# Chunk inputs laid out by neighbouring groups in DRAM, loaded for two groups in one run, with a third buffer for them and for the S5 tables

## The chip, the cores and the metric

One core of one Trainium2 chip runs the whole program in one launch. The metric is the device time in microseconds (us) of one execution. Engines are named as in the profile: PE (TensorE matmul), PEld (its weight load), DVE (VectorE), ACT (ScalarE), POOL (GpSimd), SP (SyncE, which here only issues DMAs). A DMA that SP or ACT issues is carried by up to 16 DMA engines; they are called lanes here.

## The reference: what is computed

One layer of a hybrid block on 2048 tokens of width 1024, with 256 context tokens as a prefix. The part around the change is the S5 branch:

```
z = (rmsnorm(h) * (1 + sc) + sh) @ w_in          # split into u_s5, g_s5, u_lru, g_lru
u: 1024 channels = 64 groups of 16               # S5 groups, state 64, two directions
h_t = abar * h_(t-1) + bbar u_t                  # complex scan, forward and backward, from the context's state
y = Re(C h) + d * u ;  y = gelu(y) ;  y = y * sigmoid(y @ w_glu + b_glu)
out = h + gt * ([y_s5 * silu(g_s5), y_lru * silu(g_lru)] @ w_out), then a final rmsnorm
```

All inputs and the output are float32.

## The kernel before

The S5 scan is done in chunks of T = 16 tokens: 2304 tokens are NCH = 144 chunks. Per group of 16 channels the kernel needs the chunk inputs u (128 partitions = 16 channels by 8 positions, for two halves `kt` of a chunk, 144 chunks), a table `wt` that takes a chunk's inputs to its state, a table `et` that takes states to outputs, and a table `mt` that takes a chunk's inputs to its outputs directly.

The program runs in these stages, with times of the profiled execution:

- `projections(0, ...)`, to about 600 us: matmuls of the input projection for the context and the first half of the tokens (lines 248 to 250 in `mm3`, tile `pp`), eight blocks of 128 channels for each of four kinds. Woven into it are the tables of the S5 branch, which go to DRAM: `ED`, `KD`, and `WD` (line 661, stored by POOL for two groups at a time). A block of kind `u_s5` copies its results into `zsc` (context, 16 chunks) and `zst` (64 chunks), and SP stores them to the DRAM tensor `ZU` (lines 330 and 348, two DMAs each, one for each `kt`). `zst` has one buffer: the next block's first copy into it waits until both stores have landed. The eight blocks of `u_s5` lie at about 247 to 385 us.
- `projections(1, ...)`, to about 1113 us, for the second half of the tokens, with the RG-LRU branch (`lru`) beside it. Its eight `u_s5` blocks lie at about 837 to 955 us.
- `s5_inputs` for groups 0 to 31 (`sin[0]`) and 32 to 63 (`sin[1]`), about 982 to 1146 us, woven into the last projections. For each group: four products with `wt` and u into `pw` (line 743), then four ACT copies into the scan's tile z (lines 746 to 750).
- `s5_scan`, 144 steps of three DVE instructions (lines 771, 773, 775), one scan for each half of the groups. The first needs all of `sin[0]`.
- `s5_outputs` for each half of the groups, about 1226 to 1441 us: ACT copies the states into `h` (lines 800, 801), PE makes `py` from u with `mt` (line 806) and from `h` with `et` (line 808). `out_lru` (tile `po`) is woven into the scans and the outputs as side work of PE.
- `glu` and `tail`, the last 370 us.

Each engine executes its instructions in program order, SP among them: a DMA whose buffer is not yet free keeps back all later DMAs of SP. The order of the instructions on an engine follows the generators that `merge` interleaves, with priorities from the scheduling layer. `load_u` (line 754) loads the inputs of four groups by two DMAs into one of two buffers; `wt` and `et` (tag `t2`, lines 736 and 788) are loaded for two groups at a time into one of two buffers. So the table of groups 4 and 5 can start to load when PE is done with groups 0 and 1.

The layout in DRAM: `ZU` is [2, 1024 channels, 8, 144], so one partition's inputs of four groups are four runs of 576 bytes. `WD` is [64, 128, 512], two runs of 2 KB for two groups.

Of the kernel before, what the change touches and what calls it, by code (L numbers as in the profile page):

```python
# [9 lines left out]
F32 = mybir.dt.float32  # L10
# [6 lines left out]
P = 128  # L17
D = 1024
# [5 lines left out]
G = 64  # L24
NCH = 144
T = 16
# [20 lines left out]
class Block:  # L47
# [204 lines left out]
    def projections(self, half, kinds):  # L252

        nc = self.nc
        win = self.io["w_in"].rearrange("o (k p) n -> p (o k) n", p=P)
        base = {"u_s5": 0, "g_s5": D, "u_lru": 2 * D, "g_lru": 3 * D}

        kept = {"u_lru": 0, "g_lru": 8, "u_s5": 16}

        def load(i):  # L260

            if i >= len(blocks):
                return None
            kind, b = blocks[i][:2]
            if half and kind in kept:
                w = self.wp.tile([P, 2, KT, P], F32R, tag="w", bufs=2, name="w")
                nc.sync.dma_start(out=w.rearrange("p s k n -> p (s k n)").bitcast(F32), in_=self.WS[kept[kind] + b])
                return w
            cs = base[kind] + b * P
            return self.wload(win[:, :, cs:cs + P])  # L270

        def split(raw, i):
            kind, b, tiles = blocks[i]
            if half and kind in kept:
                return raw
            with self.tc.high_priority(offset=250):
                w = self.wsplit(raw, nc.scalar.copy)
            if not half and kind in kept and tiles[-1] == both[-1]:
                nc.gpsimd.dma_start(out=self.WS[kept[kind] + b], in_=w.rearrange("p s k n -> p (s k n)").bitcast(F32))
            return w  # L280

        both = [2 * half, 2 * half + 1]
        blocks = []
        for group in kinds:
            if group == ("g_s5",) and half:
                blocks += [("g_s5", b, [t]) for t in both for b in range(8)]
            else:
                blocks += [(kind, b, ["c"] + both if half == 0 and kind[0] == "u" else both)
                           for b in range(8) for kind in group]
        if half == 0:  # L290
            blocks.remove(("g_lru", 0, both))
            blocks[:1] = [("u_lru", 0, ["c", 0]), ("g_lru", 0, [0]), ("u_lru", 0, [1]), ("g_lru", 0, [1])]
        raw, nxt = self.first if half == 0 else (load(0), None)
        w = split(raw, 0)
        raw = nxt or load(1)
        for i, (kind, b, tiles) in enumerate(blocks):
            whi, wlo = w[:, 0], w[:, 1]
            r = slice(b * P, (b + 1) * P)
            if kind == "u_lru" and tiles[0] != 1:
                u = self.conv_input(half, b)  # L300
            if kind == "u_s5":
                st = self.stp.tile([P, T, 64], F32, tag="st4", bufs=1, name="zst")
            for tl in tiles:
                n = 256 if tl == "c" else 512
                xh, xl = self.xh[tl]
                ps = self.psM.tile([P, 512], F32, tag="mm", name="pp")
                for k in range(KT):
                    self.mm3(ps[:, :n], lambda k: whi[:, k, :], lambda k: wlo[:, k, :],
                             lambda k: xh[:, k, :n], lambda k: xl[:, k, :n], (k,))
                    if k < KT - 1:  # L310
                        yield
                if kind == "u_lru":
                    pos = 1 if tl == "c" else (3 if half else LC + 4) + tl % 2 * 512
                    nc.scalar.copy(out=u[:, pos:pos + n], in_=ps[:, :n])  # L314
                    if tl == "c":
                        self.conv(half, b, u, 0)
                elif kind == "g_lru":
                    o = self.stp.tile([P, 512], F32, tag="st2", bufs=2, name="ust")
                    if half:
                        nc.scalar.activation(out=o, in_=ps, func=AF.Sigmoid)  # L320
                        nc.vector.tensor_mul(out=o, in0=ps, in1=o)
                    else:
                        nc.scalar.activation(out=o, in_=ps, func=AF.Silu)
                    nc.scalar.dma_start(out=self.GL[r, tl * 512:tl * 512 + 512], in_=o)
                elif kind == "u_s5":
                    if tl == "c":
                        sc = self.stp.tile([P, T, 16], F32, tag="st2", bufs=2, name="zsc")
                        nc.scalar.copy(out=sc[:, ::-1, :], in_=ps[:, :256].rearrange("p (c j) -> p j c", j=T))
                        for kt in range(2):
                            nc.sync.dma_start(out=self.ZU[kt, r, :, 0:16], in_=sc[:, kt * 8:kt * 8 + 8, :])  # L330
                    else:
                        o = (tl % 2) * 32
                        nc.scalar.copy(out=st[:, ::-1, o:o + 32], in_=ps.rearrange("p (j r) -> p j r", j=T))
                else:
                    o = self.stp.tile([P, 512], F32, tag="st2", bufs=2, name="gst")
                    nc.scalar.activation(out=o.rearrange("p (j a r) -> p a j r", j=8, a=2),
                                         in_=ps.rearrange("p (a j r) -> p a j r", a=2, j=8), func=AF.Silu)
                    nc.scalar.dma_start(out=self.GS[tl, r].rearrange("d j c -> d (j c)"), in_=o)
                if tl == tiles[0] and i + 1 < len(blocks):
                    w = split(raw, i + 1)  # L340
                    raw = load(i + 2)
                yield
            if kind == "u_lru" and tiles[-1] == both[-1]:
                self.conv(half, b, u)
            if kind == "u_s5":
                cs = slice(80, NCH) if half else slice(16, 80)
                for kt in range(2):
                    nc.sync.dma_start(out=self.ZU[kt, r, :, cs], in_=st[:, kt * 8:kt * 8 + 8, :])


    def conv_input(self, half, b):
# [266 lines left out]
    def s5_tables(self, tp):  # L618

        nc, v = self.nc, self.nc.vector  # L620
# [29 lines left out]
        def transposed(gp, W):  # L650
            Wt = tp.tile([P, 2, 2, 2, P], F32, tag="Wt", bufs=2, name="Wt")
            for g in range(2):
                ps = self.psT.tile([P, 512], F32, tag="t", name="psw")
                for kt in range(2):
                    for c in range(2):
# [2 lines left out]
                                            W[:, kt, g, c].rearrange("p h j -> p (h j)"),  # L658
                                            self.ident)
                nc.scalar.copy(out=Wt[:, g].rearrange("p k c m -> p (k c m)"), in_=ps)  # L660
            nc.gpsimd.dma_start(out=self.WD[2 * gp:2 * gp + 2].rearrange("g p a -> p g a"),
                                in_=Wt.rearrange("p g k c m -> p g (k c m)"))

        def lags(gq, E):

# [60 lines left out]
    def s5_inputs(self, gp, zt, hb):  # L726

        nc = self.nc
        for gl in range(32):
            g = hb * 32 + gl  # L730
            gi = gl % 2
            if gl % 4 == 0:
                u4 = self.load_u(gp, g)
            u = u4[:, :, gl % 4]
            if gi == 0:
                w = gp.tile([P, 2, 2, 2, P], F32, tag="t2", bufs=2, name="wt")
                nc.sync.dma_start(out=w.rearrange("p g k c m -> p g (k c m)"),
                                  in_=self.WD[g:g + 2].rearrange("g p a -> p g a"))
            ps = self.psM.tile([P, 512], F32, tag="mm", name="pw")
            pw = ps[:, :2 * NCH].rearrange("p (c n) -> p c n", c=2)  # L740
            for c in range(2):
# [11 lines left out]

    def load_u(self, gp, g):

        u = gp.tile([P, 2, 4, NCH], F32, tag="u", bufs=2, name="u")
        for kt in range(2):
            src = self.ZU[kt, g * 16:(g + 4) * 16].rearrange("(g h) j c -> (h j) g c", g=4)
            self.nc.sync.dma_start(out=u[:, kt], in_=src)
        return u  # L760

    def s5_scan(self, sp, zt, hb):
# [15 lines left out]
    def s5_outputs(self, gp, go, zt, hb):  # L778

        nc = self.nc  # L780
        for gl in range(32):
            g = hb * 32 + gl
            gi = gl % 2
            if gl % 4 == 0:
                u4 = self.load_u(gp, g)
            u = u4[:, :, gl % 4]
            if gi == 0:
                e = gp.tile([P, 2, 2, T, T], F32, tag="t2", bufs=2, name="et")
                src = self.ED[g // 4].rearrange("p (c a) -> p c a", c=2)[:, :, g % 4 * 256:g % 4 * 256 + 512]
                nc.sync.dma_start(out=e.rearrange("p c g j h -> p c (g j h)"), in_=src)  # L790
                ps = self.psM.tile([P, 512], F32, tag="mm", name="py")
                py = ps.rearrange("p (g a n) -> p g a n", g=2, a=2)
# [249 lines left out]
    def build(self):  # L1042
        tc, nc = self.tc, self.nc
        with ExitStack() as es:
# [4 lines left out]
            self.XC = dt("XC", [D, LC + L])  # L1049
            self.GL = dt("GL", [D, L])  # L1050
            self.YL = dt("YL", [D, L])
            self.ZU = dt("ZU", [2, D, 8, NCH])
            self.GS = dt("GS", [4, D, T, 32])
            self.YT = dt("YT", [G, T, 8, 2, P])
            self.ZD = dt("ZD", [D, 8, 2, P])
# [1 line left out]
            self.HP = dt("HP", [T, P, D])  # L1057
            self.WS = dt("WS", [24, P, 2 * KT * P])
            self.ED = dt("ED", [G // 4, P, 2048])
            self.WD = dt("WD", [G, P, 512])  # L1060
            self.KD = dt("KD", [G, T, 31, T])
            self.psM = pool(es, "psM", bufs=4, space=PSUM)
            self.psG = pool(es, "psG", bufs=2, space=PSUM)
# [152 lines left out]
```

## Time and profile before

| what | value |
|---|---|
| runs | 1814.55, 1817.27, 1821.26 us (median 1817.27) |
| profiled execution | 1820.46 us, span 1818.7 us |
| PE busy | 1703.3 us, 94% of the span |
| DVE, ACT busy | 1112.1 us (61%), 873.6 us (48%) |
| granted clock of TensorE, mean | 0.977 |
| DMA | 373.55 MB, mean 205 GB/s |

The span is the time from the first to the last instruction; 1.8 us of the profiled execution lie around it. The busy share of PE is high nearly everywhere, so time is saved mainly where PE stands still or where its clock is lower. The share of the DMA engines is the mean over the 16 lanes.

### The profile page before, as it was taken

How to read it: one execution, taken by the hardware profiler on the slowest of the kernel's cores; microseconds unless marked ns; L12 is line 12 of the kernel's file. 1: busy time of each engine (PE TensorE's matmuls, PEld its weight loads, DVE VectorE, ACT ScalarE, POOL GpSimd, SP SyncE). 2: the span in 40 equal slices, each digit the busy share in tenths (PEclk: the TensorE clock that was granted, in tenths of full speed). 3: DMA queues.
4: the chain of work that ended last, by engine and by line, in shares of the span. 5: the costliest groups of instructions: out<-in, count | busy, mean ns of one | idle time of the engine just before them, and what ended most of it. 6: DMA issues, size and time to landing. Idle time of an engine off the chain costs nothing.

```text
span 1818.7 us, 25980 instructions
## 1 busy us (share of the span) xinstructions
PE 1703.3 (94%) x9785; PEld 1365.7 (75%) x9785; DVE 1112.1 (61%) x2006; ACT 873.6 (48%) x1382; POOL 138.3 (8%) x268
## 2 busy tenths in 40 slices
PE   7787989999999899999998997989999999999997
PEld 2565777888888565656666786779988899998886
DVE  4789989985023268887667058898501166336663
ACT  2623332222365288787775888416555443222221
POOL 1022212211100000000000000000000000001121
PEclk9898999999999899999999998999999999999999
DMA  8685558877646545666777788528888757456562
GB/s 255 153 215 199 206 197 258 261 250 261 186 132 211 155 150 211 200 217 210 219 200 221 241 249 257 163 82 256 268 270 250 226 179 215 142 159 217 188 198 88
DMA packets 335470, 373.55 MB, mean 205 GB/s; under 512 B 124029, under 2 KB 274161, under 8 KB 323058
## 3 DMA queue, kind: packets, MB, share of 16 engines
q1 hardware_dynamic: 288304, 243.43, 46.9%
q0 software_dynamic: 20672, 94.91, 13.7%
q10 hardware_dynamic: 26370, 33.57, 5.3%
q8 instruction: 77, 1.26, 0.3%
q14 instruction: 47, 0.39, 0.1%
HBM read 233.49 MB, written 138.35 MB: 204 GB/s over the span
## 4 chain that ended last, share of the span: by engine, by line
PE 54%; issue 17%; DMA 11%; DVE 10%; ACT 5%; SPq 1%; POOL 1%; ACTq 0%; DVEq 0%; POOLq 0%
PE pp L248 7%; PE pp L249 7%; PE pp L250 7%; PE po L250 4%; PE po L248 4%; PE po L249 4%; PE pgl L249 3%; PE pgl L250 3%; PE pgl L248 3%; PE py L808 2%; DMA et<-ED 2%; PE py L806 2%; PE pw L743 2%; DMA wt<-WD 2%; DVE p L771 2%
## 5 line engine op out<-in xcount | busy, mean ns | idle before, releaser
L248 PE MATMUL pp<-x,w 128*128 128x512 f32 x1024 | 422.1, 413 | 13.4 <-ACT uc L314 13.0
L250 PE MATMUL pp<-x,w 128*128 128x512 f32 x1024 | 406.8, 397 | 2.6 <-DVE w L241 2.6
L249 PE MATMUL pp<-x,w 128*128 128x512 f32 x1024 | 406.8, 397 | 0.0
L248 PEld LDWEIGHTS pp<-x,w 128*128 128x128 f32 x1024 | 194.8, 190 | 114.7 <-issue 63.6
L250 PEld LDWEIGHTS pp<-x,w 128*128 128x128 f32 x1024 | 194.5, 190 | 45.3 <-DVE w L241 3.5
L249 PEld LDWEIGHTS pp<-x,w 128*128 128x128 f32 x1024 | 195.2, 191 | 37.2 <-DVE x L213 1.0
L241 DVE TENSOR_TENSOR w<-wraw,w 128x1024 fp32r<-128x1024 f32 x66 | 80.5, 1220 | 158.9 <-ACT w L240 151.4
L240 ACT CAST w<-wraw 128x1024 fp32r<-128x1024 f32 x66 | 69.1, 1047 | 142.8 <-PE pp L250 97.5
L248 PE MATMUL po<-x,w 128*128 128x512 f32 x256 | 103.3, 403 | 0.8 <-ACT z L750 0.6
L743 PE MATMUL pw<-u,wt 128*128 128x144 f32 x512 | 79.0, 304 | 23.7 <-DMA wt<-WD 16.2
L250 PE MATMUL po<-x,w 128*128 128x512 f32 x256 | 100.2, 391 | 1.0 <-DVE w L241 1.0
L249 PE MATMUL po<-x,w 128*128 128x512 f32 x256 | 99.9, 390 | 0.4 <-DVE x L839 0.4
L248 PE MATMUL po<-ws,yh 128*128 128x512 f32 x256 | 99.6, 389 | 0.0
L249 PE MATMUL po<-ws,yh 128*128 128x512 f32 x256 | 99.6, 389 | 0.0
L250 PE MATMUL po<-ws,yl 128*128 128x512 f32 x256 | 99.6, 389 | 0.0
L743 PEld LDWEIGHTS pw<-u,wt 128*128 128x128 f32 x512 | 74.4, 203 | 31.8 <-ACT z L750 12.6
L422 PE MATMUL pg<-xc,gw 64*64 64x512 f32 (+1 forms) x320 | 89.8, 581 | 8.9 <-DMA GL<-ust 8.4
L422 PE MATMUL pg<-xs,gw 64*64 64x512 f32 (+1 forms) x320 | 88.5, 581 | 4.0 <-ACT gi L426 4.0
L808 PE MATMUL py<-h,et 128*128 128x128 f32 x512 | 80.0, 280 | 12.9 <-ACT h L801 9.4
L379 DVE SCALAR_TENSOR_TENSOR xcv<-uc,vcol,xcv 128x256 f32<-128x256 f32 (+2 forms) x72 | 72.9, 1012 | 22.6 <-ACT xcv L376 21.9
L771 DVE TENSOR_TENSOR p<-z,A 128x128 f32<-128x128 f32 x288 | 77.8, 287 | 5.3
L808 PEld LDWEIGHTS py<-h,et 128*128 128x128 f32 x512 | 68.7, 195 | 14.9 <-ACT h L801 12.2
(258 smaller groups left out, 3520.5 us busy)
## 6 DMA issues: line engine op xcount, KB each, us to landing
wraw<-in_w_in_dram SPq DMA_DIRECT2D x50, 512.0 KB
WS<-w POOLq DMA_DIRECT2D x24, 1024.0 KB, 7.0
w<-WS SPq DMA_DIRECT2D x24, 1024.0 KB
u<-ZU SPq DMA_DIRECT2D x64, 288.0 KB
ED<-E POOLq DMA_DIRECT2D x16, 1024.0 KB, 5.5
WD<-Wt POOLq DMA_DIRECT2D x32, 512.0 KB, 4.3
wt<-WD SPq DMA_DIRECT2D x32, 512.0 KB
et<-ED SPq DMA_DIRECT2D x32, 512.0 KB
```

The costliest lines, as they stand in the source:

```text
L240: copy(out=w[:, 0], in_=raw)
L241: self.nc.vector.tensor_sub(out=w[:, 1], in0=raw, in1=w[:, 0])
L248: nc.tensor.matmul(ps, lhsT=whi(k), rhs=xhi(k), start=(k == 0), stop=False)
L249: nc.tensor.matmul(ps, lhsT=whi(k), rhs=xlo(k), start=False, stop=False)
L250: nc.tensor.matmul(ps, lhsT=wlo(k), rhs=xhi(k), start=False, stop=(k == KT - 1))
L379: nc.vector.scalar_tensor_tensor(out=xc, in0=u[:, o + k:o + k + N], scalar=cw[:, k * 8 + b:k * 8 + b + 1], in1=xc, op0=ALU.mult, op1=ALU.add)
L422: nc.tensor.matmul(pss[w][e * 64:e * 64 + 64, :n], lhsT=gw[ws, d, e, :], rhs=xcs[(w + e) % 2][ws, o:o + n], start=True, stop=True, tile_po ...
L743: nc.tensor.matmul(pw[:, c, :], lhsT=w[:, gi, kt, c, :], rhs=u[:, kt, :], start=(kt == 0), stop=(kt == 1))
L771: v.tensor_mul(out=p, in0=cur.unsqueeze(1).to_broadcast([P, 2, 2, 32]), in1=self.A16[:, :, :, gs])
L806: nc.tensor.matmul(o, lhsT=ms(m[:, i * 8:i * 8 + T]), rhs=u[:, i, 16:], start=(i == 0), stop=False)
L808: nc.tensor.matmul(o, lhsT=ms(e[:, i, gi]), rhs=h[:, i, :], start=False, stop=(i == 1))
```

## The change

`ZU` becomes [2, 16, 8, 64, 144]: for each channel of a group and each position in a chunk half, the 64 groups stand side by side. The stores of `zsc` and `zst` write the same bytes in the same runs of 64 and 256 bytes, addressed by group first. `load_u` loads two groups instead of four, by two DMAs with one run of 1152 bytes per partition, into one of three buffers. `WD` becomes [32, 128, 1024], one run of 4 KB per partition. `wt` and `et` get a third buffer.

```diff
-                            nc.sync.dma_start(out=self.ZU[kt, r, :, 0:16], in_=sc[:, kt * 8:kt * 8 + 8, :])
+                            nc.sync.dma_start(out=self.ZU[kt, :, :, b * 8:b * 8 + 8, 0:16].rearrange("h j g c -> g (h j) c"),
+                                          in_=sc[:, kt * 8:kt * 8 + 8, :])
...
-                    nc.sync.dma_start(out=self.ZU[kt, r, :, cs], in_=st[:, kt * 8:kt * 8 + 8, :])
+                    nc.sync.dma_start(out=self.ZU[kt, :, :, b * 8:b * 8 + 8, cs].rearrange("h j g c -> g (h j) c"),
+                                      in_=st[:, kt * 8:kt * 8 + 8, :])
...
-            nc.gpsimd.dma_start(out=self.WD[2 * gp:2 * gp + 2].rearrange("g p a -> p g a"),
-                                in_=Wt.rearrange("p g k c m -> p g (k c m)"))
+            nc.gpsimd.dma_start(out=self.WD[gp], in_=Wt.rearrange("p g k c m -> p (g k c m)"))
...
-            if gl % 4 == 0:
-                u4 = self.load_u(gp, g)
-            u = u4[:, :, gl % 4]
             if gi == 0:
-                w = gp.tile([P, 2, 2, 2, P], F32, tag="t2", bufs=2, name="wt")
-                nc.sync.dma_start(out=w.rearrange("p g k c m -> p g (k c m)"),
-                                  in_=self.WD[g:g + 2].rearrange("g p a -> p g a"))
+                u2 = self.load_u(gp, g)
+            u = u2[:, :, gi]
+            if gi == 0:
+                w = gp.tile([P, 2, 2, 2, P], F32, tag="t2", bufs=3, name="wt")
+                nc.sync.dma_start(out=w.rearrange("p g k c m -> p (g k c m)"), in_=self.WD[g // 2])
...
-        u = gp.tile([P, 2, 4, NCH], F32, tag="u", bufs=2, name="u")
+        u = gp.tile([P, 2, 2, NCH], F32, tag="u", bufs=3, name="u")
         for kt in range(2):
-            src = self.ZU[kt, g * 16:(g + 4) * 16].rearrange("(g h) j c -> (h j) g c", g=4)
-            self.nc.sync.dma_start(out=u[:, kt], in_=src)
+            src = self.ZU[kt, :, :, g:g + 2].rearrange("h j g c -> (h j) (g c)")
+            self.nc.sync.dma_start(out=u[:, kt].rearrange("p g c -> p (g c)"), in_=src)
...
-            self.ZU = dt("ZU", [2, D, 8, NCH])
+            self.ZU = dt("ZU", [2, T, 8, G, NCH])
...
-            self.WD = dt("WD", [G, P, 512])
+            self.WD = dt("WD", [G // 2, P, 1024])
```

`s5_outputs` is changed in the same way: two groups of u at a time, and three buffers for `et`.

On SP, at the start of `s5_inputs`, these DMAs stand in the kernel before (a row has the line, the tile written and read, and the shape of the side written; `wraw` are weights of the projection, `zst` the last block of chunk inputs):

```order
L759 DMA u<-ZU 128x4x144 x2
L737 DMA wt<-WD 128x2x512
L348 DMA ZU<-zst 1024x1x64 x2
L234 DMA wraw<-in_w_in_dram 128x8x128
L737 DMA wt<-WD 128x2x512
L759 DMA u<-ZU 128x4x144 x2
L234 DMA wraw<-in_w_in_dram 128x8x128 x4
L737 DMA wt<-WD 128x2x512
L234 DMA wraw<-in_w_in_dram 128x8x128 x2
L737 DMA wt<-WD 128x2x512
L759 DMA u<-ZU 128x4x144 x2
```

And in the changed kernel, at the same place of SP:

```order
L759 DMA u<-ZU 128x288 x2
L738 DMA wt<-WD 128x1024
L349 DMA ZU<-zst 8x128x64 x2
L234 DMA wraw<-in_w_in_dram 128x8x128
L759 DMA u<-ZU 128x288 x2
L738 DMA wt<-WD 128x1024
L759 DMA u<-ZU 128x288 x2
L738 DMA wt<-WD 128x1024
L234 DMA wraw<-in_w_in_dram 128x8x128 x4
L759 DMA u<-ZU 128x288 x2
L738 DMA wt<-WD 128x1024
L234 DMA wraw<-in_w_in_dram 128x8x128 x2
```

The third pair of groups now stands ahead of four loads of projection weights, and every table stands behind the inputs of its own two groups. The order of the matmuls on PE is the same in this stage.

On SP in the blocks of `u_s5` of the first half of the tokens, the stores of the chunk inputs in the kernel before:

```order
L330 DMA ZU<-zsc 1024x1x16 x2
L348 DMA ZU<-zst 1024x1x64 x2
L330 DMA ZU<-zsc 1024x1x16 x2
L234 DMA wraw<-in_w_in_dram 128x8x128
L348 DMA ZU<-zst 1024x1x64 x2
```

And in the changed kernel:

```order
L330 DMA ZU<-zsc 8x128x16 x2
L349 DMA ZU<-zst 8x128x64 x2
L330 DMA ZU<-zsc 8x128x16 x2
L234 DMA wraw<-in_w_in_dram 128x8x128
L349 DMA ZU<-zst 8x128x64 x2
```

They stand at the same places; the side written now begins with a dimension of 8 (the groups of a block) where it began with 1024.

## Rows read from the trace of the kernel before

**Rows 1.** The page's part 4: the chain that ended last, shares by engine.

```profile
PE 54%; issue 17%; DMA 11%; DVE 10%; ACT 5%; SPq 1%; POOL 1%; ACTq 0%; DVEq 0%; POOLq 0%
```

**Rows 2.** Windows: stretch, length, busy us (count) per engine; PEclk, DMA share, GB/s.

```profile
995.00:1066.00 71.00, 62.74 (x353) 54.99 (x354) 6.57 (x8) 56.75 (x132) 0.00 (x0) 0.93 0.83 247
...
1113.00:1147.00 34.00, 24.50 (x145) 22.04 (x145) 24.25 (x87) 30.82 (x73) 0.00 (x0) 0.90 0.81 255
...
1165.00:1226.00 61.00, 54.71 (x244) 44.76 (x243) 61.00 (x351) 11.18 (x16) 2.66 (x5) 0.98 0.29 95
1226.00:1331.00 105.00, 102.55 (x710) 94.96 (x711) 65.00 (x251) 63.92 (x99) 2.13 (x4) 0.98 0.85 263
...
837.00:955.00 118.00, 117.36 (x592) 70.45 (x591) 87.09 (x36) 86.27 (x100) 1.59 (x3) 1.00 0.68 195
247.00:385.00 138.00, 134.49 (x902) 109.96 (x901) 130.30 (x168) 41.30 (x77) 31.49 (x58) 0.99 0.82 248
```

**Rows 3.** Waits of PE, 995 to 1066: us in total, times, longest.

```profile
PE pw L743 <- DMA wt<-WD: 5.1, 3, 1.9
```

**Rows 4.** Waits of PE, 1066 to 1147.

```profile
PE pw L743 <- DMA wt<-WD: 11.1, 6, 2.9
```

**Rows 5.** Waits of PE, 1145 to 1450.

```profile
PE py L808 <- ACT h L801: 9.4, 2, 6.1
PE py L808 <- DMA et<-ED: 3.5, 5, 1.5
```

**Rows 6.** Timeline of PE, 1015 to 1024: start, us, instruction, count, [idle before].

```profile
1015.45 1.14 PE L743 MATMUL pw<-u,wt 128*128 128x144 f32 x8
1016.33 0.49 PE L248 MATMUL pp<-x,w 128*128 128x512 f32 x1
...
1019.23 2.18 PE L743 MATMUL pw<-u,wt 128*128 128x144 f32 x8 [1.95 <-DMA wt<-WD]
1021.03 0.80 PE L248 MATMUL pp<-x,w 128*128 128x512 f32 x1
...
1022.48 0.51 PE L248 MATMUL pp<-x,w 128*128 128x512 f32 x1
```

**Rows 7.** Waits of SP's queue, 940 to 1145.

```profile
SPq L737 <- PE pw L743: 68.7, 26, 6.2
```

**Rows 8.** Timeline of SP's queue, 1007 to 1020.

```profile
1008.25 1.02 SPq L759 DMA_DIRECT2D u<-ZU  x2
```

**Rows 9.** Waits of DVE, 1066 to 1226.

```profile
DVE x L839 <- ACT x L838: 10.3, 8, 2.8
DVE z L773 <- ACT z L747: 8.6, 1, 8.6
```

**Rows 10.** Timeline of ACT, 1216 to 1228.

```profile
1225.42 0.63 ACT L800 COPY h<-z 64x256 f32<-64x256 f32 x1 [9.29 <-DVE z L775]
```

**Rows 11.** DMA, 1000 to 1147: queue: packets, MB, share; issue: count, KB each.

```profile
q10 hardware_dynamic: 1440, 2.62, 4.8%
...
GS<-gst ACTq DMA_DIRECT2D x10, 256.0 KB
```

**Rows 12.** DMA, 1230 to 1445.

```profile
q10 hardware_dynamic: 8686, 8.38, 11.5%
...
YT<-y ACTq DMA_DIRECT2D x64, 128.0 KB
```

**Rows 13.** DMA, 402 to 472, where only `wraw` loads are on q1.

```profile
q1 hardware_dynamic: 6240, 3.15, 17.8%
```

**Rows 14.** DMA, 247 to 385.

```profile
q1 hardware_dynamic: 39520, 8.92, 31.7%
...
ZU<-zst SPq DMA_DIRECT2D x14, 256.0 KB
ZU<-zsc SPq DMA_DIRECT2D x16, 64.0 KB
```

**Rows 15.** Timeline of ACT, 875 to 884.

```profile
881.21 0.59 ACT L333 COPY zst<-pp 128x512 f32<-128x512 f32 x1 [4.20 <-DMA ZU<-zst]
```

More of the change, by code (lines that the diff above doesn't have):

```diff
@@ L783, in s5_outputs @@
             gi = gl % 2
-            if gl % 4 == 0:
-                u4 = self.load_u(gp, g)
-            u = u4[:, :, gl % 4]
             if gi == 0:
-                e = gp.tile([P, 2, 2, T, T], F32, tag="t2", bufs=2, name="et")
+                u2 = self.load_u(gp, g)
+            u = u2[:, :, gi]
+            if gi == 0:
+                e = gp.tile([P, 2, 2, T, T], F32, tag="t2", bufs=3, name="et")
                 src = self.ED[g // 4].rearrange("p (c a) -> p c a", c=2)[:, :, g % 4 * 256:g % 4 * 256 + 512]
```

## Prediction

> **What bounds the kernel now.** I read the chain first: PE has 54% of it, waits that end on a DMA 11% [rows 1]. So the path is PE's work with pieces of other things between, and what counts is where PE stands still. The windows by stage [rows 2] show where. In the outputs (1226 to 1331) PE is busy for 102.55 of 105 us: there it is the bound, and whatever is gained ahead of it carries to the end. In the inputs it stands still: 62.74 of 71 us busy in `sin[0]`'s main part, 24.50 of 34 at the end of `sin[1]`. PE's waits name the tables: `wt` ends 5.1 us of waits in 995 to 1066 [rows 3] and 11.1 us in 1066 to 1147 [rows 4], `et` 3.5 us in the outputs [rows 5]. SP's own waits say why: it waited 68.7 us in 26 pieces for PE to give a `wt` buffer free [rows 7]. With two buffers a load cannot start before the pair of groups before the running one is done, and the running pair is then all the time that it has.
>
> Two other bounds lie close by. At 1226 PE waits 6.1 us for ACT's copy of the states [rows 5]. ACT's row there shows 9.29 us idle, ended by the scan's last DVE instruction [rows 10], and DVE is busy for all of 61.00 us from 1165 to 1226 [rows 2]. So the first scan is a gate: what PE gains between the scan's start and 1226 it gives back there unless the scan ends earlier too. And at the end of `sin[1]` (1113 to 1147) ACT is busy for 30.82 of 34 us with the copies into z [rows 2], so the `wt` waits there hide little more than 3 us.
>
> **The third buffer, first half of the inputs.** The order on SP puts the third pair's loads ahead, and each later load can start two pairs ahead. That takes away the three `wt` waits, 5.1 us [rows 3]. The 1.95 us wait at 1019 was also followed by a lower clock: the eight `pw` matmuls after it took 1.80 us from start to start against 0.88 at 1015, and the next three took 1.45 us [rows 6], about twice the full-speed pace (the two levels are 1.2 and 2.4 GHz). That is 0.92 plus half of 1.45, or 1.6 us, which goes with the wait. Together 6.7 us. Can the lanes bring it? They are at 0.83 here [rows 2], or 59 us of lane time, in a stretch that would shrink to 64: 0.92. The longer runs help: one MB in runs of 512 bytes costs 12.5 us (17.8% of 70) / 3.15 = 4.0 us of all lanes [rows 13], one in runs of 2 KB 7.06 us (4.8% of 147) / 2.62 = 2.7 [rows 11]. For u, 9.4 MB here by its shape, runs of 1152 instead of 576 bytes save between 0 and 12 us; halfway, some 6 us over the whole input stage. It fits, tightly. I take 6 us gained (0 to 6.7). It carries, since the scan, which waited 8.6 us for the last copy of `sin[0]` [rows 9], starts earlier by as much.
>
> **The third buffer, second half.** PE's 11.1 us [rows 4] stand behind the gate. What moves the gate is DVE's own waiting, 10.3 us for ACT's casts of `w_out` [rows 9], which stand in ACT's queue behind the copies into z and so behind PE. ACT has 3.2 us idle at the end of the stage. I take 2 us (0 to 10.3), and expect PE's wait at 1226 to grow well beyond 6.1 us.
>
> **The third buffer, outputs.** `et` waits of 3.5 us [rows 5] with the lanes at 0.85 [rows 2]; the scan no longer gates. I take 2.5 us (0 to 3.5).
>
> **Loads in smaller pieces.** 64 more DMAs on SP, 0.51 us each [rows 8], 33 us over the inputs and outputs, on a queue that now waits for 68.7 us in the inputs alone [rows 7]: nothing, and half a microsecond in front of a table if that cover is gone. The third pair (819 KB, 3.3 us at 247 GB/s [rows 2]) now stands ahead of four weight loads on SP; those feed double-buffered weights, so I take 0 (0 to 3.3 lost). `WD` in runs of 4 KB: 0.
>
> **The stores of ZU.** They keep their 256-byte runs, but the side written now begins with a dimension of 8. Two stores of the kernel before show what that can do. Ten `GS` stores, which write 128 rows and begin with 128, left 1440 packets: 144 each, the 128 rows and 16 more [rows 11]. 64 `YT` stores, which also write 128 rows but begin with 8 on the DRAM side (`h j a c -> j h (a c)`, line 813), left 8686: 135.7 each, the rows and some 8 more [rows 12]. I read the extra packets as one for each lane that took part, so `YT` ran on 8 lanes of 16, and the new `ZU` stores will.
>
> The Trainium skill says so as a rule ("DMA: Bandwidth & Descriptors", section "Why a DMA increments its semaphore by 16 and not by 1"): the lanes are the largest number up to 16 that divides the slowest dimensions of both sides. By that rule the stores drop from 16 lanes to 8. The trace agrees, with 144 packets against 135.7.
>
> Price: in 247 to 385 q1 carries 43.7 us of lane time (31.7% of 138 [rows 14]). Its 8.92 MB are 4.72 MB of `ZU` (14 by 256 KB, 16 by 64 KB) and eight weight loads at 12.5 / 6 = 2.1 us. So `ZU` costs 27.1 us of all lanes, 3.0 us for a `zst` pair and 0.75 for a `zsc` pair. On half the lanes each pair takes twice that, and the laden lanes have 0.82 x 138 + 27.1 = 140 us of work in 138 us. What then waits is POOL's stores of tables, and ACT and DVE behind their buffers. In the second half of the tokens the lanes are at 0.68 of 118 us [rows 2]; seven `zst` pairs more on half of them make (80 + 21) / 118 = 0.86, no more than in the inputs now.
>
> From below the cost is 0: the one long wait of ACT on such a store, 4.20 us at 881 [rows 15], lies in a stage in which PE was busy for 117.36 of 118 us, so it was hidden. A gain I exclude: the same bytes go in the same runs over fewer lanes. From above, with nothing hidden, eight blocks by 3.75 us are 30 us in the first half and eight by 3.0 us 24 us in the second. I take the hidden side, which the 881 row shows, but not wholly where the laden lanes are full: 3 us lost in the first half, 1 us in the second. PE has only 3.5 us of idle in 247 to 385 to hide in, but ACT is busy for 41 of 138 us [rows 2]. Writes that lie 36.9 KB apart may cost something in the memory; no row prices that, and I put it at 0 with the same upper bound.
>
> **Sum.** 6 + 2 + 2.5 - 3 - 1 = 6.5 us gained. The profiled execution took 1820.46 us, so it would take 1814.0; the median of the runs is 3.2 us lower, at 1817.27, so the forecast is 1811.
>
> **Rivals.**
> 1. *Everything carries, stores hidden.* 6.7 + 10.3 + 3.5, about 21 us: 1797; from 12 us gained on, down to 1796 to 1805. For it: the scan's waits hang on PE, and PE hid the store at 881. Against it: ACT at 30.82 of 34 us.
> 2. *The transfers only wait elsewhere.* The lanes are at 0.81 to 0.85 already; if `wt` and `et` come no sooner because the queue ahead of them is longer, the waits stay and the stores take the little that is left: 1815 to 1820. For it: the lanes would be at about 0.9. Against: two pairs of lead instead of one. The change then doesn't do what it says.
> 3. *Slower: the stores of ZU on half the lanes.* Place: the `u_s5` blocks, the first half above all, where 140 us of work fall into 138. Price: up to 3.75 us a block. It decides once more of it is exposed than the 10.5 us gained, 1.3 us a block in the first half alone; fully exposed there it is 30 - 10.5, or 1837. I put it at 1827 to 1837. For it: DVE is busy for 130.30 of 138 us there, so the tables have no slack. Against: the 881 row.
>
> **How the numbers follow.** Forecast (2 to 11 us gained, 1806 to 1815): 0.47. Rival 1: 0.20. Rival 2: 0.17. Rival 3: 0.16. A difference under 0.5%, 9.1 us, can't be told from none: faster means under 1808.2, slower over 1826.4. Faster: rival 1 and 0.14 of the forecast, 0.34. Slower: rival 3, 0.16. The rest, 0.50, is within. The range leaves out the best third of rival 1 and two thirds of rival 3: 1799 to 1829; the forecast's own is 1806 to 1815.
>
> **What would show it.** Right: no `wt` waits of PE in `sin[0]`, the scan's first step some 6 us earlier after the start of `sin[0]`, PE's wait for ACT's `h` at the first output longer than 6.1 us, `et` waits under 1.5 us. The stores: some 8 extra packets each, ACT waiting longer for `ZU` and `WD` to land in 247 to 385, PE's idle time there grown by about 3 us. Wrong: `wt` waits of PE that stay at 10 us or more, a first scan that ends no earlier, or an idle PE in the `u_s5` blocks that outweighs the inputs.

## The result: slower by 1.1%

The changed kernel took 1838.35 us (median of 4 runs, 1833.59 to 1845.51) against 1819.26 for the kernel before on the same chip: ratio 1.0111, 95% interval 1.0082 to 1.0140. The forecast was 1811 us with a range to 1829. What came is the mechanism of the third rival, the stores of `ZU` on half the lanes; the time lies just beyond the 1837 us at which that rival ended.

Three groups of matmuls divide the time between the stages. In the profiled executions (1820.46 us before, 1833.59 after) the first and the last start of the products of `s5_inputs` (line 743) and of the second product of `s5_outputs` (line 808), and the first gates of the RG-LRU branch (`pg`), with min/median/max duration in ns ahead of them, were before:

```profile
L422 PE MATMUL pg<-xc,gw x320: 375/589/1112, 624.4 to 946.4; 64*64 64x512 f32 x128, 64*64 64x256 f32 x32
L743 PE MATMUL pw<-u,wt x512: 283/286/608, 982.3 to 1141.1; 128*128 128x144 f32 x171
L808 PE MATMUL py<-h,et x512: 272/275/580, 1226.7 to 1440.1; 128*128 128x128 f32 x171
```

and after:

```profile
L424 PE MATMUL pg<-xc,gw x320: 376/589/1113, 636.9 to 969.1; 64*64 64x512 f32 x128, 64*64 64x256 f32 x32
L743 PE MATMUL pw<-u,wt x512: 283/286/609, 1005.6 to 1153.4; 128*128 128x144 f32 x171
L808 PE MATMUL py<-h,et x512: 273/275/579, 1242.8 to 1453.4; 128*128 128x128 f32 x171
```

At the first gates, behind the first half of the tokens, the changed kernel is 12.5 us late. The inputs start 23.3 us late, the outputs start 16.1 us late and end 13.3 us late. So the stage of the first half lost 12.5 us and that of the second 10.8; inputs and first scan gave back 7.2, the outputs 2.8. The gains came to 10.0 us, where the forecast's terms make 10.5. The losses came to about 23 us where it put 4.

These sums compare one execution of each kernel. The two lie 13.1 us apart, the medians 19.1, so the typical loss is larger than the profiles show. Other profiled executions tell how far the stages scatter: in the seven whose stores begin with 1024 and whose splits are as before (the kernel before and runs 1 and 7 to 11) the first gates come at 618.2 to 624.4 us and the inputs at 978.6 to 982.5; in the changed kernel and runs 2 and 5, whose stores begin with 8, at 633.1 to 636.9 and 1000.0 to 1007.2.

The windows of the kernel after (columns as in [rows 2]), for the `u_s5` blocks of the first and the second half:

```profile
247.00:398.00 151.00, 136.34 (x895) 110.59 (x894) 124.08 (x163) 38.34 (x75) 25.82 (x51) 0.95 0.74 214
855.00:978.00 123.00, 118.01 (x576) 68.70 (x575) 83.31 (x36) 84.92 (x98) 1.60 (x3) 0.97 0.64 176
```

The first row holds about the matmuls of the 138 us stretch before [rows 2]. PE's idle time in it grew from 3.5 to 14.7 us, its clock fell from 0.99 to 0.95, and the mean share of the lanes fell from 0.82 to 0.74 although ACT waits for a DMA. Lanes that are idle beside lanes that are full would look like this, but the profile shows only the mean of the 16, not a single lane.

ACT's waits in 245 to 400 (us, times, longest) name the transfer. Before, `zst` waits were 5.2 us in the whole program.

```profile
ACT zst L334 <- DMA ZU<-zst: 52.2, 5, 13.0
ACT zsc L328 <- DMA ZU<-zsc: 18.5, 4, 6.6
ACT kk L683 <- DMA ZU<-zsc: 16.0, 1, 16.0
```

ACT's timeline shows four of the five places, with the idle time in brackets:

```profile
330.55 0.59 ACT L334 COPY zst<-pp 128x512 f32<-128x512 f32 x1 [12.96 <-DMA ZU<-zst]
346.40 0.59 ACT L334 COPY zst<-pp 128x512 f32<-128x512 f32 x1 [11.07 <-DMA ZU<-zst]
368.85 0.59 ACT L334 COPY zst<-pp 128x512 f32<-128x512 f32 x1 [12.60 <-DMA ZU<-zst]
385.28 0.59 ACT L334 COPY zst<-pp 128x512 f32<-128x512 f32 x1 [10.33 <-DMA ZU<-zst]
```

The fifth, of 5.27 us, ends at 308.85. So five of the eight blocks wait, for 5 to 13 us. The chain of the stretch 340 to 390 has two stores as its longest pieces (start, us):

```profile
352.26 16.50 DMA ZU<-zst
...
371.74 13.45 DMA ZU<-zst
```

Behind ACT's wait stand its copies of the tables (`Wt`) and its first half of the weight split (`w`), and behind these DVE and PE. PE's waits in 247 to 398 were before:

```profile
PE psw L657 <- DVE W L627: 3.0, 2, 2.6
```

and after:

```profile
PE psw L659 <- DVE W L629: 7.6, 2, 5.4
PE psw L659 <- ACT Wt L662: 6.6, 2, 5.2
```

PE's timeline at the end of ACT's last wait, with the idle time and its releaser in brackets:

```profile
386.41 1.97 PE L659 MATMUL psw<-ident,W 128*128 128x128 f32 x8 [5.24 <-ACT Wt L662]
...
390.19 0.79 PE L248 MATMUL pp<-x,w 128*128 128x512 f32 x1
390.79 0.63 PE L249 MATMUL pp<-x,w 128*128 128x512 f32 x1
391.21 0.61 PE L250 MATMUL pp<-x,w 128*128 128x512 f32 x1
391.64 0.42 PE L248 MATMUL pp<-x,w 128*128 128x512 f32 x1
391.90 0.40 PE L249 MATMUL pp<-x,w 128*128 128x512 f32 x1
392.13 0.39 PE L250 MATMUL pp<-x,w 128*128 128x512 f32 x1
```

After 5.24 us of rest the big matmuls start 0.60, 0.42 and 0.43 us apart, and then 0.26 and 0.23. The granted clock was 0.50 from 386 to 391.6 and 0.99 from 391.6 to 396: the lower of the two levels (1.2 GHz) for over 5 us, on top of the wait.

SP pays too. Issuing a `zst` store took 0.61 us in the median before and 2.18 after (min/median/max in ns). Before:

```profile
L348 SPq DMA_DIRECT2D ZU<-zst x32: 513/614/2775, 271.9 to 956.1; - x32
```

After:

```profile
L349 SPq DMA_DIRECT2D ZU<-zst x32: 572/2183/6921, 269.2 to 978.8; - x32
```

After, SP's queue between 336 and 371 has next to no free time, and the weight loads stand in it:

```profile
336.82 12.85 SPq L330 DMA_DIRECT2D ZU<-zsc  x2
349.77 0.99 SPq L234 DMA_DIRECT2D wraw<-in_w_in_dram  x1
350.86 8.32 SPq L349 DMA_DIRECT2D ZU<-zst  x2
359.28 4.70 SPq L234 DMA_DIRECT2D wraw<-in_w_in_dram  x1
364.07 6.62 SPq L330 DMA_DIRECT2D ZU<-zsc  x2
```

In the second half a part of the loss comes through SP: PE waited 3.81 us at 904.31 for `xc`, whose load SP issued at 896.56, right behind a pair of stores that took 3.20 us to issue (1.28 before). That wait, not there before, makes up most of PE's idle time in the blocks: 5.0 us in 855 to 978 against 0.6 in [rows 2]. From the first gates to the inputs PE stood still 4.1 us longer, and the same matmuls (1732 and 1733) kept it busy for 357.46 us against 350.78. Of these 6.7 us, 3.6 are there in run 1 as well (354.38 us, with the old layout), so that they are no price of the stores; the rest stays open.

The waits of PE in 1000 to 1165 and in 1165 to 1460, which answer to [rows 3 to 5]:

```profile
PE pw L743 <- ACT z L750: 10.1, 3, 6.1
PE pw L743 <- DMA wt<-WD: 6.0, 3, 3.8
...
PE py L808 <- ACT h L801: 8.6, 5, 4.0
```

`wt` went from 16.2 us in nine waits to 6.0 in three, `et` went from 3.5 to none; ACT's copies into z took the place of part of it.

### The profile page after: what moved, and what is told of

Same layout as the page of the kernel before. It is cut to its first block, busy times and chain, and to the rows that moved or that the text cites. A ratio compares the mean times of both kernels' runs of the same rounds, so it can differ in the third digit from the quotient of the medians.

```text
span 1831.8 us, 26073 instructions
## 1 busy us (share of the span) xinstructions
PE 1714.7 (94%) x9785; PEld 1370.4 (75%) x9785; DVE 1113.1 (61%) x2006; ACT 873.3 (48%) x1382; POOL 132.1 (7%) x268
## 4 chain that ended last, share of the span: by engine, by line
PE 53%; issue 19%; DMA 11%; DVE 9%; ACT 6%; SPq 1%; POOL 1%; ACTq 0%; DVEq 0%; POOLq 0%
PE pp L248 6%; PE pp L249 6%; PE pp L250 6%; PE po L249 4%; PE po L250 4%; PE po L248 4%; PE pgl L249 3%; PE pgl L250 3%; PE pgl L248 3%; PE py L808 2%; PE py L806 2%; PE pw L743 2%; DMA ZU<-zst 2%; DVE p L771 1%; DVE xcv L381 1%
## 5 line engine op out<-in xcount | busy, mean ns | idle before, releaser
L424 PE MATMUL pg<-xc,gw 64*64 64x512 f32 (+1 forms) x320 | 94.4, 596 | 11.9 <-DMA GL<-ust 7.2
L424 PE MATMUL pg<-xs,gw 64*64 64x512 f32 (+1 forms) x320 | 93.2, 596 | 3.5 <-ACT gi L428 3.4
L743 PEld LDWEIGHTS pw<-u,wt 128*128 128x128 f32 x512 | 72.5, 198 | 23.6 <-ACT z L750 11.4
L806 PE MATMUL py<-u,mt 128*128 128x128 f32 x512 | 79.4, 278 | 0.0
```

Of the source, the lines that this page charges most:

```text
L424: nc.tensor.matmul(pss[w][e * 64:e * 64 + 64, :n], lhsT=gw[ws, d, e, :], rhs=xcs[(w + e) % 2][ws, o:o + n], start=True, stop=True, tile_po ...
L743: nc.tensor.matmul(pw[:, c, :], lhsT=w[:, gi, kt, c, :], rhs=u[:, kt, :], start=(kt == 0), stop=(kt == 1))
L806: nc.tensor.matmul(o, lhsT=ms(m[:, i * 8:i * 8 + T]), rhs=u[:, i, 16:], start=(i == 0), stop=False)
```

## The experiments

Ratios are to the kernel before on the same chip, with the 95% interval.

**1. The old layout, the rest of the change.** The changed kernel with `ZU` as it was (stores begin with 1024; two groups of u by two runs of 576 bytes):

```diff
-            self.ZU = dt("ZU", [2, T, 8, G, NCH])
+            self.ZU = dt("ZU", [2, D, 8, NCH])
```

> The changed kernel with ZU as before: the stores begin with 1024 rows again, u is loaded for two groups in two runs of 576 bytes per partition. Third buffers and WD stay changed. If the layout of ZU alone costs the 23 us that the u_s5 blocks lose (lanes or addresses), this is some 10 us faster than the kernel before, about 1809, with ACT waits for zst and zsc under 10 us. If the extra loads or the order on SP cost it, it stays above 1825.

1810.59 us, 0.9963 [0.9948, 0.9979]; `zst` waits of ACT 4.3 us in all. The layout alone costs 1.5%, about 27 us by the ratios, and the rest of the change gains 3.8 to 9.4.

**2. Lanes or addresses?** The kernel before with 576 bytes of padding after each group, so that group and channel can't be folded and the store begins with 8, at addresses as close together as before:

```diff
-            self.ZU = dt("ZU", [2, D, 8, NCH])
+            self.ZU = dt("ZU", [2, G, 129, NCH])
...
-  nc.sync.dma_start(out=self.ZU[kt, r, :, cs], ...
+  nc.sync.dma_start(out=self.ZU[kt, b * 8:b * 8 + 8, 0:128, cs], ...
```

> The kernel before with 576 bytes of padding between the groups of ZU, so that the stores begin with a dimension of 8, while their addresses stay as near as before. Lanes theory (8 of 16 lanes): about 20 to 25 us slower than before, 1840 to 1845, with ACT waiting 60 us or more for zst. Address theory (writes 36.9 KB apart are slow): the same as before within 5 us, and waits of about 5 us.

1838.92 us, 1.0114 [1.0095, 1.0133], which is 17 to 24 us slower; ACT waited 57.3 us for `zst` in all. The page's packet counts, of the kernel before:

```profile
DMA packets 335470, 373.55 MB, mean 205 GB/s; under 512 B 124029, under 2 KB 274161, under 8 KB 323058
```

And of this one:

```profile
DMA packets 335086, 373.55 MB, mean 203 GB/s; under 512 B 123645, under 2 KB 273777, under 8 KB 322674
```

384 packets fewer, all of the smallest kind, the bytes the same: 48 stores of `ZU` (32 of `zst`, 16 of `zsc`) by 8. Read as in the prediction, one packet for each lane, each store left 8 lanes out, and most of the layout's 27 us is there without far addresses. By the rule cited in the prediction (the Trainium skill, "DMA: Bandwidth & Descriptors", section "Why a DMA increments its semaphore by 16 and not by 1") a side that begins with 8 gives 8 lanes beside one of 128 partitions; these counts agree.

What a pair costs by itself is seen in the second half, where it runs alone on the lanes. The busy share and GB/s in 40 slices of 0.175 us, after (855 to 862):

```profile
DMA  9854356666676676669667767655555542000000
GB/s 421 328 234 167 73 130 143 146 138 124 108 111 108 102 114 105 94 100 200 111 107 107 113 107 105 98 75 72 72 72 75 67 60 26 0 0 0 0 0 0
```

and before (841 to 848):

```profile
DMA  9999199999999999979200000000000000000000
GB/s 328 328 421 374 56 294 296 221 317 269 280 278 250 238 222 227 199 126 179 38 13 9 0 0 0 0 0 0 0 0 0 0 0 0 0 0 0 0 0 0
```

After the tail of a weight load, the pair takes 17 slices (3.0 us) before and 29 (5.1 us) after. The share after is at first 0.6 to 0.7, more than 8 of 16 lanes would give; it goes by the times of packets and comes out above 1 elsewhere (1.05 in 340 to 350 before), so it doesn't count lanes. The time is near the price of the forecast, 3.0 us and twice that. It doesn't explain landings of 13 to 17 us.

**3. Sixteen lanes at far addresses.** The changed kernel with the channels of a block in another order, so that the stores begin with 128 and one partition's two groups are still one run; the order is made where DVE and ACT split the weights of `u_s5`, by reading them with a stride:

```diff
+        if swap:
+            raw = raw.rearrange("p k (g h) -> p k h g", g=8)
...
-            self.ZU = dt("ZU", [2, T, 8, G, NCH])
+            self.ZU = dt("ZU", [2, 8, 8, T, 8, NCH])
```

> The changed kernel with the channels of a block in another order (channel of the group outermost, by splitting the weights of u_s5 in that order), so that the stores begin with 128 rows while a partition's eight runs lie 590 KB apart and u is still loaded in one run of 1152 bytes. Lanes theory: some 10 us faster than before, 1806 to 1811. Address theory: as slow as the changed kernel, about 1838.

1819.77 us, 1.0018 [1.0003, 1.0034]; `zst` waits 3.9 us. The lanes are back and the waits gone, but 9 us more than run 1 are left.

**4. The strided split alone.** Run 1 with the split of run 3 (the channels inside a block come out in another order than the reference's):

> The kernel with ZU as before and third buffers, with only the strided weight split of e3_perm added for u_s5; this leaves the S5 channels inside a block in the wrong order, everything else is done. If what e3_perm lost against e1_old_zu (9 us) is DVE's strided split in a stage in which DVE has no slack, this is about 1819 too. If it is the far addresses of the stores and loads of ZU, this is about 1811.

1818.37 us, 1.0001 [0.9990, 1.0012]. The split took 1309 ns in the mean, against 1220 in run 1 (busy us, mean ns, idle time before). Here:

```profile
L245 DVE TENSOR_TENSOR w<-wraw,w 128x1024 fp32r<-128x1024 f32 x66 | 86.4, 1309 | 158.7 <-ACT w L244 145.7 <-DMA u<-ZU 13.0
```

In run 1:

```profile
L241 DVE TENSOR_TENSOR w<-wraw,w 128x1024 fp32r<-128x1024 f32 x66 | 80.5, 1220 | 154.4 <-ACT w L240 154.4
```

Eight strided splits cost some 6 us of DVE, in the stage where DVE is busy for 130 of 138 us [rows 2], and by the ratios the split costs 0.0038 of the time, some 7 of run 3's 10 us. What is left for far addresses and longer loads together is 0.0017 of the time, some 3 us, and the two intervals touch.

**5. A second buffer for `zst`.** The changed kernel, every other block of the first half in an idle buffer:

```diff
+                if b % 2 and not half:
+                    st = self.ucp.tile([P, 1024], F32, tag="xcv", bufs=1, name="zst")...
```

> The changed kernel, but in the first half of the tokens every second block of u_s5 puts zst into another buffer (one of the convolution's, which is idle there), so that a block no longer waits for the stores of the block before. If the loss passes through the single zst buffer (ACT waits, and PE's transposes behind ACT), most of the 16 us lost in the first half comes back: about 1825. If it passes through the full lanes (every store of tables lands late), little comes back: 1833 or more.

1828.1 us, 1.0062 [1.0043, 1.0082]: by the medians some 9 us come back of the changed kernel's loss, and all four runs lie under its four, though the intervals meet. The profiled execution, the slowest of the four at 1833.55 us, shows nothing of it: its first gates come at 636.8 us, those of the changed kernel at 636.9. ACT's waits in 240 to 410:

```profile
ACT zsc L331 <- DMA ZU<-zsc: 32.3, 3, 16.5
ACT kk L686 <- DMA ZU<-zsc: 20.5, 2, 16.1
```

ACT no longer waits there for a store of `zst` (56.7 us in the changed kernel), but for `zsc` 32.3 us instead of 18.5. With the buffer freed, the wait goes to the next store that ACT depends on. So the single buffer is likely a part of the loss, which one profile that shows no gain doesn't settle, and not all of it.

**6. Without POOL's stores of split weights.** The changed kernel, in which the weights of `u_s5` are not stored to DRAM by POOL in the first half (8 stores of 1 MB), but loaded and split again in the second:

```diff
-        kept = {"u_lru": 0, "g_lru": 8, "u_s5": 16}
+        kept = {"u_lru": 0, "g_lru": 8}
```

> The changed kernel without POOL's stores of the split u_s5 weights in the first half (8 MB in its u_s5 blocks); the second half loads and splits them again. If the stores of ZU take 12 us and more in the first half because POOL's stores share the laden lanes, the ACT waits for zst there fall from 52 us to under 30 and the stage 250 to 398 shortens by 5 us or more. If 8 lanes alone set it, both stay.

1828.83 us (a single run). The window 247 to 398:

```profile
247.00:398.00 151.00, 147.88 (x1008) 121.41 (x1007) 138.91 (x182) 45.19 (x84) 25.67 (x51) 1.00 0.74 198
```

ACT's waits for `zst` in 245 to 400:

```profile
ACT zst L334 <- DMA ZU<-zst: 18.0, 3, 8.3
```

Stores on 8 lanes all the same, but PE is busy for 147.88 of 151 us at a granted clock of 1.00, against 136.34, the waits fell from 52.2 to 18.0 us, and the first gates come at 618.8 us, no later than with 16 lanes. The first half's loss needs POOL's large stores beside the stores on 8 lanes. (A few of ACT's copies stand at other places here. The second half pays for its own splits: 384.1 us from the first gates to the inputs, against 368.7. What POOL's stores cost the kernel before stays open.)

**7. Where the gain is from: two buffers for the tables.** Run 1 with `wt` and `et` back at two buffers:

```diff
-  w = gp.tile([P, 2, 2, 2, P], F32, tag="t2", bufs=3, name="wt")
+  w = gp.tile([P, 2, 2, 2, P], F32, tag="t2", bufs=2, name="wt")
```

> The kernel with ZU as before (two-group loads, WD in runs of 4 KB), but with two buffers for wt and et again. If the third buffer is what gains, this is as the kernel before, 1815 to 1820, with wt waits of PE of 14 us or more. If the larger runs of WD and the order on SP gain, it stays near 1810.

1807.87 us, 0.9959 [0.9941, 0.9976]. As fast as run 1: the third buffer of the tables, to which the forecast gave all of its gain, gives nothing that can be measured once u comes in smaller pieces. PE still waited 13.7 us for `wt`. In the profiled executions the third buffer did bring the scan's first step forward (78.7 us behind the start of the inputs in run 1, 82.5 here), but the outputs took 214.8 us with it and 207.8 without; whether that is the buffer or scatter was not separated, and what a third buffer does beside u in pieces of four groups stays open.

**8 and 9. `WD` alone, and the loads of u alone.** The kernel before with each of the two other parts:

```diff
+            nc.gpsimd.dma_start(out=self.WD[gp], in_=Wt.rearrange("p g k c m -> p (g k c m)"))
```
```diff
-        u = gp.tile([P, 2, 4, NCH], F32, tag="u", bufs=2, name="u")
+        u = gp.tile([P, 2, 2, NCH], F32, tag="u", bufs=3, name="u")
```

> The kernel before with one part of the change alone: WD stored and loaded in one 4 KB run per partition instead of two of 2 KB. Theory A (what gains in the version with two table buffers is that inputs are loaded two groups at a time, in step with the tables, so that no table stands behind 1.2 MB of inputs): no change, 1817 to 1821 us, ratio 0.998 to 1.001, and PE's waits for wt stay at about 16 us. Rival B (the longer runs of WD are what gains: the tables land sooner): 1811 to 1814 us, and the waits for wt fall below 10 us.

> The kernel before with the other part alone: inputs loaded two groups at a time into three buffers, by two runs of 576 bytes per partition; ZU, WD and the two buffers of wt and et as before. Theory A (the smaller loads of inputs are what gains): 1809 to 1813 us, ratio 0.994 to 0.997, first step of the outputs some 5 to 7 us earlier after the start of the inputs than before. Rival B (the longer runs of WD gain): 1816 to 1820 us. Rival C (neither alone; the gain needs both): both kernels at 1815 to 1818.

`WD`: 1814.07 us, 0.9997 [0.9982, 1.0011]. Loads of u: 1809.27 us, 0.9964 [0.9946, 0.9981]. The loads of u in pieces of two groups account for the whole gain of run 1.

**10 and 11. Two and four buffers for these pieces.**

```diff
-        u = gp.tile([P, 2, 2, NCH], F32, tag="u", bufs=3, name="u")
+        u = gp.tile([P, 2, 2, NCH], F32, tag="u", bufs=2, name="u")
```

> The kernel before with inputs loaded two groups at a time, as in the run that gained 6 us alone, but into two buffers instead of three. Theory A (what gains is that a table never stands behind more than one pair's inputs on the queue): still 1808 to 1813 us, ratio 0.994 to 0.997. Rival B (what gains is the third buffer, which lets the inputs run a pair ahead): 1817 to 1825 us, and PE waits for DMA u<-ZU appear.

> The kernel before with inputs loaded two groups at a time into four buffers (the same memory as its two buffers of four groups); tables with two buffers. Three buffers took 1809.3 us where two took 1823.7. Theory A (with three the loads are far enough ahead, and what is left are ACT's copies into z, 25 us of PE's waits, and the scan): 1806 to 1811 us, ratio 0.993 to 0.997. Rival B (the smaller pieces on the queue matter more than the lead, so a fourth buffer gives as much again as its share): 1798 to 1804 us. Rival C (loads running further ahead put inputs in front of the tables on the queue again): 1812 to 1818 us, and PE's waits for wt back at 14 us or more.

Two: 1823.74 us, 1.0042 [1.0027, 1.0057]. Four: 1810.47 us, 0.9966 [0.9948, 0.9983]. SP's waits in 940 to 1145 (us, times, longest), with three buffers:

```profile
SPq L737 <- PE pw L743: 57.3, 25, 6.9
```

With two:

```profile
SPq L759 <- PE pw L743: 67.2, 28, 6.4
```

With three, what SP waits for is a table's buffer (line 737). With two it is a buffer of u (759), and the table stands behind it. The time is lost in the outputs, though, where SP waits in the same way: with two, 44.3 us for a buffer of u that the products with `mt` (line 806) still read, a wait that is not there with three. The second product of the outputs ran from 1220.2 to 1430.5 us with three and from 1220.7 to 1446.6 with two: the third buffer earns its 14 us there. The windows of 1226 to 1440 with three:

```profile
1226.00:1440.00 214.00, 210.65 (x1421) 191.77 (x1420) 69.67 (x238) 119.14 (x188) 4.78 (x9) 1.00 0.86 261
```

With two:

```profile
1226.00:1440.00 214.00, 202.61 (x1348) 184.92 (x1348) 70.08 (x240) 116.04 (x183) 4.25 (x8) 0.97 0.84 251
```

PE stands still for 11.4 us instead of 3.4, and its clock is lower. Its waits name the tables and hardly u: 6.0 us for `et` (1.6 with three), 1.5 for `mt`, 0.2 for u.

**12. The stores by group.** The changed kernel with sixteen stores of `zst` a block, one for each group and `kt`, so that both sides begin with 16:

```diff
+                for gg in range(8):
+                    for kt in range(2):
+                        nc.sync.dma_start(out=self.ZU[kt, :, :, b * 8 + gg, cs],
+                                          in_=st[gg * 16:gg * 16 + 16, kt * 8:kt * 8 + 8, :])
```

> The changed kernel with one edit: zst of a block is stored by sixteen DMAs, one for each group and kt, so that both sides begin with 16 (channels of the group); the addresses written, and the zsc stores, stay as in the changed kernel. Theory (half the lanes make a store slow, and two zst pairs then stand in the way of a block): 1815 to 1822 us, ACT's waits on ZU<-zst fall from 69 us to under 20, while the zsc stores still cost a little; the sixteen issues on SP, about 0.4 us each, take some 6.5 us a block. Rival A (it is the far addresses, 36.9 KB apart, that make the stores slow): 1835 us or more. Rival B (sixteen issues stand in front of the weight loads on SP and cost as much as they give): 1826 to 1834 us, with PE or ACT waiting for wraw in the u_s5 blocks.

1937.15 us, 1.0661 [1.0644, 1.0677], which no theory had. ACT's waits for `ZU<-zst` did fall, from 69.4 to 11.8 us. But the edit moved other work: the scheduling layer now put up to eight copies of `Wt` in a row ahead of `zst`, and PE waited for DVE's tables, longer than for anything else:

```profile
PE psw L660 <- DVE W L630: 51.9, 20, 9.3
```

Its time says nothing on lanes. How much of it is the order and how much the 256 issues on SP was not separated.

## Why the prediction was wrong

**The step that failed** is the price of the stores: "I take the hidden side, which the 881 row shows, but not wholly where the laden lanes are full: 3 us lost in the first half, 1 us in the second." What it rested on was right as far as it went: 8 lanes (run 2), a pair alone at somewhat under twice its 3.0 us (the slices), far addresses next to nothing (runs 3 and 4). The size was off, at about 23 us instead of 4 in the profiles and some 27 by the ratio to run 1. By stage the profiles show 12.5 us instead of 3 in the first half and 10.8 instead of 1 in the second (15.6 and 7.7 against run 1's execution).

In the first half the prediction also had the wait in part in the wrong place. It let POOL's stores of tables wait on the laden lanes, and ACT and DVE behind them. These did land later, but by little (the median from issue to landing went from 5.8 to 6.0 us for `WD` and from 5.3 to 7.4 for `ED`). The long waits were for the stores of `ZU` themselves, in ACT. The price of a pair was taken from its own bytes, but two of them took 13.45 and 16.50 us, about as long as a block of some 17 us (138 by eight), which one buffer can't hide. ACT's wait stands ahead of the tables that ACT, PE and DVE exchange, and the idle PE then ran at its lower clock. Run 6 shows the condition: without POOL's stores of split weights the first half lost nothing in its one execution. That a pair waits on its lanes for what is ahead of it is the likely reason, argued from that run and from the prediction's own 140 us of lane work in 138; no view shows it for a single lane. The second buffer (run 5) may be worth some 9 us.

In the second half the row at 881 [rows 15] was the wrong guide for another reason. It is of this very stage, and the lanes were not full there (0.68 [rows 2]). But a wait that is hidden at the old price need not be hidden at a higher one: ACT's waits for `zst` grew from 4.2 us in one to 12.7 in five, SP's later loads came late, and PE waited where it had not. The prediction had the overfull lanes as a number and still chose between its ends (0 and 30) by that row.

**The gains** came to 10.0 us in the profile, where 10.5 were forecast: 7.2 against 8 for inputs and scan, 2.8 against 2.5 for the outputs. No `wt` wait of PE was left in `sin[0]`, and the scan's first step came 6.2 us earlier after the start of the inputs (79.4 us against 85.6), as forecast. The cause was wrong, and so the agreement of the sums is in part luck: run 1, the same change with the old layout, gained 3.8 to 9.4 us in all. The third buffer of the tables is worth nothing measurable in time (run 7), though SP's 68.7 us of waits for it [rows 7] are real: a queue may wait for a buffer that nobody needs sooner. What gains is u in smaller pieces (run 9), which the forecast had priced at 0 as 64 more DMAs, and only with more than two buffers (runs 10 and 11).

**The scan as a gate** held: by run 1's rows the last product of the inputs was at 1130.4 us, in run 7 at 1135.5, yet the first outputs came at 1218.1 and 1219.8. The changed kernel too gained 11.0 us within the inputs and had 7.2 of them at the first outputs. But the sign that the forecast named for it did not come: PE's wait for ACT's `h` at the first output was to grow well beyond 6.1 us, and it was 4.0 (8.6 us in five waits, against 9.4 in two). **`WD`** at 0: right (run 8).

**The chances.** The rival that came had 0.16, for the 881 row against it. Its own text held what decides: DVE without slack, and an exposure of 1.3 us a block as the point from which it loses. Its price, up to 3.75 us in each block, was too low for a block that waits (5 to 13 us). The range up to 1829 left out four fifths of that rival's 1827 to 1837, not two thirds. The last of the signs that were to show it wrong came: PE's idle time in the `u_s5` blocks of both halves grew by 15.5 us (11.2 and 4.3), more than inputs and outputs gained.

## To carry to other kernels

Look at which dimension comes first on both sides of a DMA whenever a layout changes: longer runs for the reader can halve the lanes of the writer. Price such a store by the load that is already on its lanes and by how many buffers stand behind it, not by its own bytes, and don't take a wait that is hidden at the old price as hidden at a higher one. When a queue waits for a buffer, ask whether its consumer waits as well before giving it another one; here the versions with u in pieces of two groups, three or four buffers for it and the old layout are the fastest (runs 1, 7, 9 and 11, 1807.87 to 1810.59 us, not to be told apart), and the larger runs were not needed.

## What the hardware showed that was not expected

The issue of a store on SP slowed with its lanes: two `zsc` stores, 64 KB each, took up to 12.85 us to issue, where such a pair took 1.53 to 6.28 us before. A DVE subtraction of 128 by 1024 values took up to 1986 ns in run 4, where eight of 66 read and write with a stride; in run 1 none took more than 1227.
